# Output projection of a two-layer trunk: half columns of the gate loaded and summed piece by piece

## The chip, the cores and the metric

The kernel runs on one core of one Trainium2 chip. The metric is the device time of one execution in microseconds (us); lower is better. In the profile PE is the matrix engine, PEld its weight loads, DVE the vector engine, ACT the scalar engine, POOL the GpSimd engine, and SP the engine whose queue issues most transfers. Every engine works through its own instructions in a fixed order.

## The reference, cut to what matters

One sequence of 512 tokens with 2048 channels passes through two layers, an mLSTM layer and a band-attention layer, all in float32. Each layer ends in the same way; the part that the change touches is the end of the second one:

```python
sc = silu(c)                                            # (1, 2048)
mod = sc @ ada_w[l] + ada_b[l]                          # three blocks of 2048
shift, scale, gate = mod[:, :D], mod[:, D:2*D], mod[:, 2*D:]
...
y = (o * silu(z)) @ w_out                               # (512, 2048) @ (2048, 2048)
x = x + gate * rmsnorm(y, g_post[l])
```

So the last stage has two independent jobs: the product with `w_out`, and the gate of 2048 values, a matrix-vector product with 2048 x 2048 weights (16 MB). They meet where the product is multiplied with the gate, scaled by the row's norm and added to x.

## The kernel before

Products run on PE in float32 split into a high and a low part: each product of 128 x 128 by 512 columns is three matmuls. The weights come as pieces of 128 x 1024 (512 KB). `raw_load` issues a piece's load on SP into one of three buffers (`wr`, L259); `split` makes the high part with a cast on ACT and the low part with a subtraction on DVE, into one of three pairs (`wh`, L243). The subtraction ends the use of the load's buffer, so that the load of the piece three further on waits for it; the cast waits until PE is done with the piece three before.

The last stage (from L1552 on) computes the output in four groups of 512 columns, each in four banks of 128 tokens. `proj_b` takes a group through eight pieces of weights, k = 0, 2, ... 14. In groups 0 to 2 a piece serves all four banks with 24 matmuls (two blocks k by four banks by three), and the pieces are numbers 497 to 504, 505 to 512 and 513 to 520. Group 3 goes through its columns twice, for the token pairs (0, 1) and (2, 3), with 12 matmuls a piece: pieces 521 to 528 and 529 to 536. In the last pass the final three pieces are held and used bank by bank. There are five banks for this in turn, so that a group's second bank is one that the group before has to have emptied. `evac` empties a bank: DVE multiplies it with the gate row and writes `yo` (group 0 is copied, its gate comes later), and ACT squares it for the row's norm (`sqy`).

The gate is summed on DVE. `ada_load` loads a half column block (128 x 1024 of `adaT`, 512 KB, tile `ada`) and `ada_sum` (L550) multiplies it with silu(c), which stands as `scC` in all partitions, and sums along the row into one column of `mod`; a row that reads the accumulator follows each sum. There are 16 column blocks of two halves, 32 sums, taken in the order of blocks 84 to 95 and then 80 to 83, since group 0's gate is used last. Four buffers hold half columns. When a group's four blocks are summed, `gates_out` multiplies them with the norm's weights on DVE (`ggate`, L819), PE turns them into rows (`ps_gg`, L821), ACT copies them (L823), and SP writes them to `ggd`. `gate_row` then loads the row into all partitions, as `ssum` for groups 1 to 3 and as `gb0` for group 0. `gate_first` multiplies group 0's four outputs with `gb0`. `fetch_x` loads the residual of 128 tokens as two transfers of 512 KB. `finish` scales, adds and stores 128 tokens (four stores of 256 KB).

`gate_steps` says at which k of which group each of these steps is written into the program. Within an engine a scheduler may place an instruction earlier or later than the program does, by a priority, except that loads and sums of half columns keep their place among themselves and their neighbours roughly as written; the order that results is fixed when the program is built. Before, `gate_sums` works four half columns at a time: it sums the four that are loaded and issues the next four loads.

Of the kernel before, what the change touches and what calls it, by code (L numbers as in the profile page):

```python
# [187 lines left out]
def hybrid_trunk(ctx, tc, xT, xN, c, adaT, cols, wst, wg, ext, kc, out):  # L188
# [621 lines left out]
    def add_at(at, more):  # L810
        for k, f in more.items():
            at[k] = f if k not in at else lambda f=f, g=at[k]: (g(), f())
# [768 lines left out]
    def finish(m):  # L1581
        rs = row_rstd(m)
        if m in last:
            last[m]()
        for g in range(4):
            y = yo[m][g]
            nc.vector.scalar_tensor_tensor(y, y, rs, x2[m][g], op0=ALU.mult, op1=ALU.add)
            nc.sync.dma_start(out[m, :, g * S : (g + 1) * S], y)

    late, last = [], {}  # L1590
    gate_cols = [(80 + i, j) for i in [*range(4, KT), *range(4)] for j in range(2)]
    gate_in = []

    def gate_begin():
        late.append(op.tile([P, D], F32, tag="sc", name="scC", bufs=1))
        late.append(op.tile([P, S], F32, tag="gb", name="gb0", bufs=1))
        nc.sync.dma_start(late[0], csc.rearrange("a d -> (a d)").partition_broadcast(P))
        gate_sums()

    def gate_sums():  # L1600

        for a in gate_in:
            ada_sum(*a, tc.keep_in_program_order, late[0])
        gate_in[:] = [ada_load(i, op, 4, tc.keep_in_program_order, 2, [j]) for i, j in gate_cols[:4]]
        del gate_cols[:4]

    def gate_part(g):
        gates_out(1, 4 * g, 4 * g + 4, rp, bufs=1)

    def gate_first():  # L1610

        for m in range(4):
            nc.vector.tensor_tensor(yo[m][0], yo[m][0], late[1], op=ALU.mult)

    gate_steps = {
        0: {10: gate_begin},
        1: {0: gate_sums, 4: gate_sums, 8: lambda: gate_part(1), 10: gate_sums, 12: lambda: (gate_row(1, 1), fetch_x(0)), 14: gate_sums},
        2: {2: lambda: (gate_part(2), gate_sums()), 4: lambda: fetch_x(1), 6: lambda: (gate_row(1, 2), gate_sums()), 10: gate_sums, 12: lambda: (gate_part(3), fetch_x(2)), 14: gate_sums},
        3: {2: lambda: (gate_row(1, 3), fetch_x(3)), 4: lambda: gate_part(0), 8: lambda: gate_row(1, 0, late[1]), 12: gate_first},
    }  # L1620
    for g in range(4):
        for pair in [range(4)] if g < 3 else PAIRS:
            ps = [newp(f"ps_y1_{g}_{m}") for m in pair]
# [6 lines left out]
                    evac(p, m, g, yo[m][g], g > 0, last if g == 3 and pair == PAIRS[1] else None)  # L1630
    finish(2)
    finish(3)
    assert wpos[0] == len(order)
    ost.close()


# [57 lines left out]
```

## Time and profile before

| what | value |
|---|---|
| device time, three runs | 2645.3 us median (2644.92 to 2646.06) |
| the profiled execution | 2643.96 us, its span 2642.0 us |
| mean granted clock of PE | 0.996 |
| DVE, ACT, POOL busy | 88%, 54%, 2% of the span |
| stage of the last projection | PE's first `ps_y` of it at 2451.19 us, its last group of products from 2628.35 us |
| in that stage, PE waits by releaser | ACT `sqy` 3.2 us (2), DVE `wh` 1.6 us (2), ACT `wh` 0.3 us (1) |
| in that stage, DVE waits for half columns | 24.1 us in 12 waits; a sum takes 1.28 us |
| in that stage, ACT's casts wait for weights | 17.2 us in 9 waits |

The span runs from the first to the last instruction; the device time is measured around it. A row of the timeline has the start and the length in us, the engine, the line, the operation with its tiles and the number of instructions merged into it, and in brackets how long the engine was idle before it and what ended the wait. A row of busy time by stretches has, behind the stretch, its length, the busy time of PE, PEld, DVE, ACT and POOL with instruction counts, the granted clock, the busy share of the DMA engines and GB/s.

### The profile page before, as it was taken

Reading aid. Unit: us, or ns where it says so; the run is one execution under the profiler, and the core shown is the slowest. Engines: PE = TensorE matmul, PEld = TensorE weight load, DVE = VectorE, ACT = ScalarE, POOL = GpSimd, SP = SyncE. Lnnn points to the kernel's source line nnn. Section 1 sums busy time; section 2 is a strip of 40 time slices with the busy share of each in tenths; the row PEclk is TensorE's granted clock in tenths of the full one; section 3 lists DMA queues with packets and bytes.
Section 4 is the critical chain, followed back from the end, with each engine's and each line's share of the span. In section 5 each row is a group of like instructions: output and inputs, shape, how many; then the busy total and the mean of one; then the engine's idle time right before and its main releaser. Section 6 shows DMA issues by size and latency. Waiting matters only on the chain.

```text
span 2642.0 us, 45758 instructions
## 1 busy us (share of the span) xinstructions
PE 2579.1 (98%) x17994; PEld 2409.5 (91%) x17994; DVE 2337.3 (88%) x3812; ACT 1438.0 (54%) x2113; POOL 55.1 (2%) x110
## 2 busy tenths in 40 slices
PE   8999999999999999999999999999999999999998
PEld 6887888899999999999999998788999899999887
DVE  8978988999989999899998886877997999999666
ACT  4344533466556665566655453578443776677423
POOL 0000111000000000000000000000000000000000
PEclk9999999999999999999999999999999999999999
DMA  9766797433333333333337548878654534444687
GB/s 365 310 266 247 273 347 294 171 111 127 110 99 126 120 116 119 101 127 120 111 122 248 185 162 318 308 253 307 223 174 143 169 125 140 144 132 141 228 309 241
DMA packets 155825, 510.60 MB, mean 193 GB/s; under 512 B 17893, under 2 KB 31749, under 8 KB 141145
## 3 DMA queue, kind: packets, MB, share of 16 engines
q1 hardware_dynamic: 145498, 445.99, 49.2%
q0 software_dynamic: 10112, 61.70, 6.3%
q8 instruction: 141, 2.31, 0.4%
q14 instruction: 74, 0.61, 0.1%
HBM read 473.96 MB, written 38.90 MB: 194 GB/s over the span
## 4 chain that ended last, share of the span: by engine, by line
PE 57%; DVE 22%; issue 9%; DMA 7%; ACT 4%; POOL 0%; SPq 0%; DVEq 0%; ACTq 0%; POOLq 0%
DVE wh L243 6%; PE ps_azo L311 4%; PE ps_dzo L311 4%; PE ps_czo L311 4%; DVE ada L550 4%; PE ps_y_True L311 3%; PE ps_dz L311 3%; PE ps_cz L311 3%; PE ps_az L311 3%; PE ps_y L311 3%; PE ps_y_False L311 3%; DMA wr<-in_wst 2%; DMA ada<-in_adaT 2%; PE ps_bzo L311 2%; PE ps_s L311 2%
## 5 line engine op out<-in xcount | busy, mean ns | idle before, releaser
L243 ACT CAST wh<-wr 128x1024 fp32r<-128x1024 f32 (+1 forms) x536 | 553.4, 1034 | 453.0 <-DMA wr<-in_wst 97.5
L243 DVE TENSOR_TENSOR wh<-wr,wh 128x1024 fp32r<-128x1024 f32 (+1 forms) x536 | 644.4, 1205 | 118.0 <-ACT wh L243 117.2
L243 ACT CAST wsh<-ws 128x768 fp32r<-128x768 f32 (+1 forms) x296 | 241.7, 817 | 314.7 <-PE ps_az L311 67.4
L243 DVE TENSOR_TENSOR wsh<-ws,wsh 128x768 fp32r<-128x768 f32 (+1 forms) x296 | 277.6, 938 | 48.8 <-ACT wsh L243 48.1
L550 DVE CUSTOM_DVE_ANT_0 ada<-ada,scB,cl 128x2048 f32<-128x2048 f32 (+1 forms) x89 | 206.1, 2325 | 12.2 <-DMA ada<-in_adaT 11.8
L282 DVE TENSOR_TENSOR ws<-wr 128x512 f32<-128x512 f32 (+1 forms) x296 | 199.3, 675 | 6.2 <-DMA wr<-in_wst 5.8
L311 PE MATMUL ps_y<-wh,y 128*128 128x512 f32 x768 | 171.6, 384 | 5.2 <-ACT sqy L1161 3.2
L311 PE MATMUL ps_y_False<-wh,y 128*128 128x512 f32 x768 | 169.1, 381 | 3.0 <-DVE wh L243 2.7
L311 PEld LDWEIGHTS ps_y<-wh,y 128*128 128x128 f32 x768 | 145.0, 191 | 28.4 <-ACT sqy L1161 4.0
L311 PEld LDWEIGHTS ps_y_False<-wh,y 128*128 128x128 f32 x768 | 144.2, 189 | 25.7 <-DVE wh L243 5.0
L311 PE MATMUL ps_v<-wh,h 128*128 128x512 f32 x576 | 127.5, 380 | 0.0
L311 PE MATMUL ps_kv<-wh,hkv 128*128 128x512 f32 x576 | 126.5, 380 | 0.8 <-DVE wh L243 0.8
L284 DVE TENSOR_TENSOR ws<-wr 128x256 f32<-128x256 f32 (+1 forms) x296 | 122.8, 417 | 3.4
L283 DVE TENSOR_TENSOR wr<-ws,wr 128x256 f32<-128x256 f32 (+1 forms) x296 | 122.5, 416 | 2.5
L311 PEld LDWEIGHTS ps_kv<-wh,hkv 128*128 128x128 f32 x576 | 108.0, 189 | 17.0 <-DVE wh L243 1.8
L311 PEld LDWEIGHTS ps_v<-wh,h 128*128 128x128 f32 x576 | 108.2, 189 | 15.8 <-issue 0.9
L311 PE MATMUL ps_l<-h,wh 128*128 128x512 f32 x480 | 107.8, 380 | 2.1 <-DVE wh L243 2.1
L311 PEld LDWEIGHTS ps_l<-h,wh 128*128 128x128 f32 x480 | 90.2, 189 | 16.8 <-DVE wh L243 3.3
L311 PE MATMUL ps_azo<-h,wh 128*128 128x256 f32 (+1 forms) x606 | 92.9, 285 | 0.0
L311 PE MATMUL ps_y_True<-wh,y 128*128 128x512 f32 x384 | 83.3, 379 | 0.0
L311 PEld LDWEIGHTS ps_y_True<-wh,y 128*128 128x128 f32 x384 | 72.5, 189 | 10.3
L550 DVE CUSTOM_DVE_ANT_0 ada<-ada,scC,cl 128x2048 f32<-128x2048 f32 (+1 forms) x35 | 65.2, 1863 | 18.8 <-DMA ada<-in_adaT 18.8
(431 smaller groups left out, 5853.5 us busy)
## 6 DMA issues: line engine op xcount, KB each, us to landing
wr<-in_wst SPq DMA_DIRECT2D x506, 512.0 KB, 3.5
ada<-in_adaT POOLq DMA_DIRECT2D x57, 1024.0 KB, 7.1
ada<-in_adaT SPq DMA_DIRECT2D x49, 1024.0 KB, 7.0
ada<-in_adaT SPq DMA_DIRECT2D x36, 512.0 KB, 7.7
wr<-in_wst SPq DMA_DIRECT2D x26, 384.0 KB, 3.7
xt<-nsc SPq DMA_DIRECT2D x32, 256.0 KB, 3.6
yr<-ysc SPq DMA_DIRECT2D x28, 256.0 KB, 5.7
ysc<-zo SPq DMA_DIRECT2D x24, 256.0 KB, 4.1
```

The source lines that it names most:

```text
L243: ins = nc.scalar.copy(hi, src), nc.vector.tensor_tensor(lo, src, hi.bitcast(F32), op=ALU.subtract)
L282: nc.vector.tensor_tensor(t[:, : 2 * w], r[:, w : 3 * w], r[:, : 2 * w], op=ALU.subtract)
L283: nc.vector.tensor_tensor(r[:, w : 2 * w], t[:, w : 2 * w], r[:, :w], op=ALU.add)
L284: nc.vector.tensor_tensor(t[:, 2 * w :], r[:, 3 * w :], r[:, w : 2 * w], op=ALU.subtract)
L311: product[0] = nc.tensor.matmul(ps, a, b, start=start, stop=stop)
L550: pin(nc.vector.tensor_tensor_reduce(c, c, (sc or scB)[:, j * w : (j + 1) * w], 1.0, mod[:, i : i + 1] if j else col(CB + i), ALU.mult, AL ...
```

## The change

The 32 half columns are taken one at a time. `gate_sums(n)` does n steps; a step sums the oldest half column if four are under way (or if none is left to load) and issues one load. The first load comes at the second piece of group 0 (`gate_begin` moves from k = 10 to k = 2), and then one step follows per piece in group 0, one or two per piece in groups 1 and 2 (two where k is a multiple of 4), and 2, 2 and 1 in the first three pieces of group 3. The other steps move by one or two pieces, as `gate_steps` shows; `gate_first` multiplies two of group 0's outputs at k = 12 and two at k = 14. The stores of the first 256 tokens go from SP to POOL.

```diff
-            nc.sync.dma_start(out[m, :, g * S : (g + 1) * S], y)
+            (nc.gpsimd if m < 2 else nc.sync).dma_start(out[m, :, g * S : (g + 1) * S], y)
...
         nc.sync.dma_start(late[0], csc.rearrange("a d -> (a d)").partition_broadcast(P))
-        gate_sums()
-
-    def gate_sums():
-
-        for a in gate_in:
-            ada_sum(*a, tc.keep_in_program_order, late[0])
-        gate_in[:] = [ada_load(i, op, 4, tc.keep_in_program_order, 2, [j]) for i, j in gate_cols[:4]]
-        del gate_cols[:4]
+
+    def gate_sums(n=1):
+
+        for _ in range(n):
+            if len(gate_in) == 4 or not gate_cols:
+                ada_sum(*gate_in.pop(0), tc.keep_in_program_order, late[0])
+            if gate_cols:
+                i, j = gate_cols.pop(0)
+                gate_in.append(ada_load(i, op, 4, tc.keep_in_program_order, 2, [j]))
...
-    def gate_first():
-
-        for m in range(4):
+    def gate_first(m0):
+
+        for m in range(m0, m0 + 2):
             nc.vector.tensor_tensor(yo[m][0], yo[m][0], late[1], op=ALU.mult)
...
-        0: {10: gate_begin},
-        1: {0: gate_sums, 4: gate_sums, 8: lambda: gate_part(1), 10: gate_sums, 12: lambda: (gate_row(1, 1), fetch_x(0)), 14: gate_sums},
-        2: {2: lambda: (gate_part(2), gate_sums()), 4: lambda: fetch_x(1), 6: lambda: (gate_row(1, 2), gate_sums()), 10: gate_sums, 12: lambda: (gate_part(3), fetch_x(2)), 14: gate_sums},
-        3: {2: lambda: (gate_row(1, 3), fetch_x(3)), 4: lambda: gate_part(0), 8: lambda: gate_row(1, 0, late[1]), 12: gate_first},
+        0: {2: gate_begin},
+        1: {6: lambda: gate_part(1), 10: lambda: gate_row(1, 1), 12: lambda: fetch_x(0)},
+        2: {2: lambda: gate_part(2), 6: lambda: (gate_row(1, 2), fetch_x(1)), 12: lambda: (gate_part(3), fetch_x(2))},
+        3: {2: lambda: (gate_row(1, 3), fetch_x(3)), 6: lambda: gate_part(0), 8: lambda: gate_row(1, 0, late[1]), 12: lambda: gate_first(0), 14: lambda: gate_first(2)},
     }
+    for k in range(2, KT, 2):
+        add_at(gate_steps[0], {k: gate_sums})
+    for g in (1, 2):
+        gate_steps[g] = {k: lambda n=1 + (k % 4 == 0), f=gate_steps[g].get(k): (gate_sums(n), f and f()) for k in range(0, KT, 2)}
+    for k, n in ((0, 2), (2, 2), (4, 1)):
+        gate_steps[3][k] = lambda n=n, f=gate_steps[3].get(k): (gate_sums(n), f and f())
```

What the scheduler makes of it is seen in the order of instructions on each engine, at three places. In the names, `ada92_0` is the first half of column block 92, `wh515` the split of piece 515, `yo2_1` the output of token block 2 in group 1, and the number at a tile's end is its own. The rows that read the accumulator after each sum are left out.

On DVE at the end of group 1, before the change, from the split of piece 514 to that of 515:

```order
L243 TENSOR_TENSOR wh514_27615<-wr514_27613,wh514_27615 128x1024
L1158 TENSOR_TENSOR yo0_1_27546<-ps_y1_1_0_27251,ssum_108 128x512
L1158 TENSOR_TENSOR yo1_1_27550<-ps_y1_1_1_27252,ssum_108 128x512
L550 ISA ada92_0_27509,mod_103<-ada92_0_27509,scC_27113,cl_100 128x1024
L1158 TENSOR_TENSOR yo2_1_27554<-ps_y1_1_2_27253,ssum_108 128x512
L550 ISA ada92_1_27511,mod_103<-ada92_1_27511,scC_27113,mod_103 128x1024
L1158 TENSOR_TENSOR yo3_1_27558<-ps_y1_1_3_27254,ssum_108 128x512
L243 TENSOR_TENSOR wh515_27648<-wr515_27646,wh515_27648 128x1024
```

and after it, up to the gate product for columns 88 to 91:

```order
L243 TENSOR_TENSOR wh514_27609<-wr514_27607,wh514_27609 128x1024
L1158 TENSOR_TENSOR yo0_1_27543<-ps_y1_1_0_27260,ssum_108 128x512
L1158 TENSOR_TENSOR yo1_1_27547<-ps_y1_1_1_27261,ssum_108 128x512
L550 ISA ada93_0_27512,mod_103<-ada93_0_27512,scC_26965,cl_100 128x1024
L1158 TENSOR_TENSOR yo2_1_27551<-ps_y1_1_2_27262,ssum_108 128x512
L1158 TENSOR_TENSOR yo3_1_27555<-ps_y1_1_3_27263,ssum_108 128x512
L550 ISA ada91_1_27440,mod_103<-ada91_1_27440,scC_26965,mod_103 128x1024
L243 TENSOR_TENSOR wh515_27644<-wr515_27642,wh515_27644 128x1024
L550 ISA ada92_0_27473,mod_103<-ada92_0_27473,scC_26965,cl_100 128x1024
L819 TENSOR_TENSOR ggate_105<-mod_103,cl_100 128x4
```

One sum is left between the evictions instead of two, and it is of another half column. Before, the gate product stood ahead of the split of 513; now it stands behind that of 515. On SP the load of `ada92_0` stood right behind the load of piece 516, with those of `ada92_1` and `ada93_0` behind it; now the load of `ada93_0` stands alone right behind the load of piece 515.

On DVE at the end of group 2, before the change, from the last two sums on:

```order
L550 ISA ada83_0_27754,mod_103<-ada83_0_27754,scC_27113,cl_100 128x1024
L550 ISA ada83_1_27756,mod_103<-ada83_1_27756,scC_27113,mod_103 128x1024
L819 TENSOR_TENSOR ggate_105<-mod_103,cl_100 128x4
L243 TENSOR_TENSOR wh522_27901<-wr522_27899,wh522_27901 128x1024
L1158 TENSOR_TENSOR yo0_2_27859<-ps_y1_2_0_27562,ssum_108 128x512
L1158 TENSOR_TENSOR yo1_2_27863<-ps_y1_2_1_27563,ssum_108 128x512
L1158 TENSOR_TENSOR yo2_2_27867<-ps_y1_2_2_27564,ssum_108 128x512
L1158 TENSOR_TENSOR yo3_2_27871<-ps_y1_2_3_27565,ssum_108 128x512
L243 TENSOR_TENSOR wh523_27924<-wr523_27922,wh523_27924 128x1024
```

and after it, from the last eviction of group 2 to the same gate product:

```order
L1158 TENSOR_TENSOR yo3_2_27864<-ps_y1_2_3_27562,ssum_108 128x512
L550 ISA ada81_1_27744,mod_103<-ada81_1_27744,scC_26965,mod_103 128x1024
L243 TENSOR_TENSOR wh523_27918<-wr523_27916,wh523_27918 128x1024
L550 ISA ada82_0_27776,mod_103<-ada82_0_27776,scC_26965,cl_100 128x1024
L243 TENSOR_TENSOR wh524_27941<-wr524_27939,wh524_27941 128x1024
L550 ISA ada82_1_27779,mod_103<-ada82_1_27779,scC_26965,mod_103 128x1024
L243 TENSOR_TENSOR wh525_27959<-wr525_27957,wh525_27959 128x1024
L550 ISA ada83_0_27821,mod_103<-ada83_0_27821,scC_26965,cl_100 128x1024
L550 ISA ada83_1_27871,mod_103<-ada83_1_27871,scC_26965,mod_103 128x1024
L243 TENSOR_TENSOR wh526_27976<-wr526_27974,wh526_27976 128x1024
L819 TENSOR_TENSOR ggate_105<-mod_103,cl_100 128x4
```

Five sums and four splits have moved in between the last eviction and the gate product. On SP the load of `ada83_1`, the last half column, now stands behind the load of piece 526, which stands behind the load of `ssum` for group 3 and the first half of the residual of token block 3.

On PE in group 3 the transpose of that gate product stood, before, between pieces 522 and 523:

```order
L311 MATMUL ps_y1_3_0_27875<-wh522_27901,y2_1_1_26975 128x512 x3
L311 MATMUL ps_y1_3_1_27876<-wh522_27901,y2_1_1_26975 128x512 x3
L821 MATMUL ps_gg1_0_27917<-kcs_101,ggate_105 4x128
L311 MATMUL ps_y1_3_0_27875<-wh523_27924,y2_2_0_27009 128x512 x3
L311 MATMUL ps_y1_3_1_27876<-wh523_27924,y2_2_0_27009 128x512 x3
```

and stands after it within piece 525:

```order
L311 MATMUL ps_y1_3_0_27868<-wh524_27941,y2_3_1_27058 128x512 x3
L311 MATMUL ps_y1_3_1_27869<-wh524_27941,y2_3_1_27058 128x512 x3
L311 MATMUL ps_y1_3_0_27868<-wh525_27959,y2_4_0_27094 128x512 x3
L821 MATMUL ps_gg1_0_27934<-kcs_101,ggate_105 4x128
L311 MATMUL ps_y1_3_1_27869<-wh525_27959,y2_4_0_27094 128x512 x3
```

It has moved from 24 matmuls into group 3 to 51. At the end, on DVE, the split of piece 532 moves from behind the first two multiplies of `finish` to ahead of them; between the splits of 534 and 535 stood three of these multiplies before, and stand a reciprocal and three multiplies after the change.

More of the change, by code (lines that the diff above doesn't have):

```diff
@@ L1632, in hybrid_trunk @@
     finish(3)
-    assert wpos[0] == len(order)
+    assert wpos[0] == len(order) and not gate_cols and not gate_in
     ost.close()
```

## The prediction

> **What bounds the kernel now.** I read the page first, for the share of each engine.
>
> ```profile
> PE 2579.1 (98%) x17994; PEld 2409.5 (91%) x17994; DVE 2337.3 (88%) x3812; ACT 1438.0 (54%) x2113; POOL 55.1 (2%) x110
> ```
>
> PE is busy for 98% of the span, so a change that removes no matrix product can win only what PE loses in waits. I then read busy time by stretches, the stage before the changed one (2400 to 2450 us) beside the changed one.
>
> ```profile
> 2400.00:2450.00 50.00, 50.00 (x433) 49.68 (x433) 47.49 (x107) 35.16 (x65) 0.00 (x0) 1.00 0.50 152
> 2500.00:2550.00 50.00, 46.99 (x218) 40.66 (x218) 35.50 (x52) 12.69 (x21) 0.00 (x0) 1.00 0.84 292
> 2550.00:2600.00 50.00, 49.81 (x224) 42.76 (x223) 33.08 (x45) 14.77 (x24) 0.00 (x0) 0.97 0.87 294
> 2600.00:2642.00 42.00, 31.63 (x141) 25.94 (x139) 29.41 (x43) 15.28 (x23) 0.00 (x0) 0.96 0.65 217
> ```
>
> Up to 2450 us PE has no gap. In the last stage it loses about 3 us between 2500 and 2550, and the granted clock falls to 0.97 after it; DMA is busy 84 and 87% there against 50% before. The timeline of PE alone says where. In it a row's matmuls are counted, and the start of the next row shows what they really took.
>
> ```profile
> 2466.70 54.23 PE L311 MATMUL ps_y<-wh,y 128*128 128x512 f32 x250
> 2520.79 24.85 PE L311 MATMUL ps_y<-wh,y 128*128 128x512 f32 x114
> 2548.65 1.77 PE L311 MATMUL ps_y<-wh,y 128*128 128x512 f32 x6 [3.01 <-ACT sqy L1161]
> 2550.29 27.62 PE L311 MATMUL ps_y<-wh,y 128*128 128x512 f32 x120
> 2577.77 11.90 PE L311 MATMUL ps_y<-wh,y 128*128 128x512 f32 x54
> 2589.87 4.15 PE L311 MATMUL ps_y<-wh,y 128*128 128x512 f32 x18 [0.19 <-ACT sqy L1161]
> 2593.88 30.20 PE L311 MATMUL ps_y<-wh,y 128*128 128x512 f32 x138
> 2624.40 0.48 PE L311 MATMUL ps_y<-wh,y 128*128 128x512 f32 x1 [0.31 <-ACT wh L243]
> 2625.66 1.92 PE L311 MATMUL ps_y<-wh,y 128*128 128x512 f32 x6 [0.78 <-DVE wh L243]
> 2628.35 5.23 PE L311 MATMUL ps_y<-wh,y 128*128 128x512 f32 x23 [0.78 <-DVE wh L243]
> ```
>
> The undisturbed pace comes from the first two rows: 250 products in 2520.79 - 2466.70 = 54.1 us, 0.216 us each. Against it, from start to start: the 114 products take 27.9 instead of 24.6 us (3.2 lost); the next 6 + 120 take 29.1 instead of 27.2 (1.9 lost); the 54 and the 18 lose 0.5 together; the 138, 1, 6 and 23 at the end lose 0.7 + 1.0 + 1.4 + 0.3 = 3.4. That is 9.0 us in all, the ceiling of any gain in this stage, unless what follows the last product shrinks too. The second loss is the clock:
>
> ```profile
> 2545.50:2548.60 3.10, 0.14 (x1) 0.00 (x0) 2.62 (x4) 0.69 (x2) 0.00 (x0) 1.00 1.01 412
> 2550.30:2553.00 2.70, 2.70 (x9) 2.15 (x8) 2.67 (x4) 1.36 (x4) 0.00 (x0) 0.50 0.70 214
> ```
>
> An idle stretch of about 3 us (2545.6 to 2548.65) is followed by a granted clock of 0.50 for 2.7 us, in which 9 products run instead of 12. So the middle gap costs 3.2 + 1.9 = 5.1 us.
>
> [...] The row decides for this execution, and I keep 5.1.
>
> What PE waits for at the middle gap stands on DVE, ACT and SP:
>
> ```profile
> 2531.64 0.33 SPq L259 DMA_DIRECT2D wr<-in_wst  x1
> 2537.22 1.37 SPq L544 DMA_DIRECT2D ada<-in_adaT  x3
> ...
> 2539.44 0.68 DVE L1158 TENSOR_TENSOR yo<-ps_y,ssum 128x512 f32<-128x512 f32 x1
> 2545.98 1.28 DVE L550 CUSTOM_DVE_ANT_0 ada<-ada,scC,cl 128x1024 f32<-128x1024 f32 x1 [5.86 <-DMA ada<-in_adaT]
> 2547.19 0.69 DVE L1158 TENSOR_TENSOR yo<-ps_y,ssum 128x512 f32<-128x512 f32 x1
> 2547.91 0.58 ACT L1161 ACTIVATE sqy<-ps_y 128x512 f32<-128x512 f32 x1 [5.02 <-DVE yo L1158]
> ```
>
> The eviction of group 1's third bank (2547.19) stands on DVE behind a column sum, which waits 5.86 us for its half column: issued first of three at 2537.22, landed at 2545.98, 8.7 us. PE's group 2 needs that bank for its fourth product chain, after 18 products.
>
> **The change, part by part.** No product, sum, split or byte is added or removed; 32 half-column loads, 32 sums and 8 output stores move.
>
> *Sums from the second piece on.* At the middle gap the half column between the evictions is now 93's first half, and its load stands on SP right behind wr515, which waits for the split of piece 512. Before, that place was reached at 2531.64 (the row above), so at that pace the load is issued at about 2532.1, 5.2 us earlier than the one it replaces. Even with the same 8.7 us it lands at 2540.8. DVE reaches the sum when the second eviction ends (2539.44 + 0.68 = 2540.1); PE needs the bank 18 products into group 2, at 2545.5; sum and eviction take 1.3 + 0.6, and PE went on 0.7 after the square began (2547.91, 2548.65). So the sum may start as late as 2542.8, and the gap goes: **-5.1 us**, with the bounds 0 and -5.1. What is late next is a new one. PE's transpose of gate columns 88 to 91 keeps its place, 24 products into group 2 (2546.8), but its operand now comes behind the sum of 93, two evictions, a second sum, a split and a third sum: 3 x 1.3 + 2 x 0.6 + 1.2 + 0.1 = 6.4 us after the first starts, 2547.2 from 2540.8. Taken as **+0.3 us**, bounds 0 and 2.
>
> The two small losses at the start of group 3 (0.5) come from group 2's evictions, which before stood behind two waiting sums. In the new order three splits stand ahead of them and no sum: **-0.4**.
>
> *Five sums after group 2.* Before, all sums and the last gate product of DVE end before group 2 does. Now five sums stand between the last eviction of group 2 and the last gate product, with four splits among them, and PE's last transpose stands 51 products into group 3, in order, with products behind it.
>
> ```profile
> 2500.24 0.69 DVE L1160 COPY yo<-ps_y 128x512 f32<-128x512 f32 x1 [0.60 <-PE ps_y L311]
> 2573.69 1.28 DVE L550 CUSTOM_DVE_ANT_0 ada<-ada,scC,cl 128x1024 f32<-128x1024 f32 x1
> 2576.23 1.22 DVE L243 TENSOR_TENSOR wh<-wr,wh 128x1024 fp32r<-128x1024 f32 x1
> 2587.18 0.16 DVE L819 TENSOR_TENSOR ggate<-mod,cl 128x4 f32<-128x4 f32 x1
> ...
> 2593.86 0.27 PE L821 MATMUL ps_gg<-kcs,ggate 128*4 128x128 f32 x1
> ```
>
> Let T be the start of group 3 on PE. The last eviction ends at about T + 0.7 (as at group 0, first row). Five sums with their accumulator reads are 5 x 1.30, four splits 4 x 1.20, so the gate product is done at T + 12.1; PE stands at the transpose at T + 51 x 0.216 = T + 11.0. It waits **1.1 us at least**; before, the operand was 6.7 us ahead (2587.18 against 2593.86). The last of the five sums also needs its load. On SP that load stands behind the load of ssum, which waits for the last eviction, behind 512 KB of x and behind wr526, which waits for the split of 523; so it is issued at T + 0.7 + 1.3 + 1.2 + 0.4 = T + 3.6, and DVE is there at T + 0.7 + 4 x 1.3 + 3 x 1.2 = T + 9.5. It has 5.9 us to land.
>
> ```profile
> DMA to landing us min/median/max: 5.6/7.7/11.7
> SPq L1150 <- DVE yo L1158: 2.0, 1, 2.0
> ...
> 2593.29 5.54 DMA wr<-in_wst
> ```
>
> The 32 loads of this stage landed after 5.6, 7.7 and 11.7 us (least, median, most). The same wr526 in the same company (ssum and x ahead of it) took 5.5 us. The new load follows wr526 directly, with fewer column loads around it than the median one had. I take 7.2 us, between the nearest row and the median: 1.3 late, so the wait is **+2.4 us**. The ends are 1.1 (5.6 us) and 6.9 (11.7 us). Above about 3 us the clock row above adds 1.6 or so.
>
> What hides the other 24 sums in groups 1 and 2: a piece lasts 24 x 0.216 = 5.2 us there, and DVE needs one split and one or two sums for it (2.5 to 3.8 us). At most four loads are under way, so one group's twelve bear a landing time of up to about 12 us. Three sums in group 0 stand in DVE's idle time of 2470 to 2490, beside splits that are wanted about 8 us later. With that cover gone (loads at the maximum), one piece would come late by a sum or two, 1 to 3 us.
>
> *First group's gating in two steps, outputs on POOL.* The four products with gb0 take the same time; three now stand ahead of the split of piece 530. The end is this:
>
> ```profile
> 2615.73 1.00 SPq L1588 DMA_DIRECT2D out<-yo  x2
> 2621.07 2.07 DVE L1587 SCALAR_TENSOR_TENSOR yo<-yo,rsn,x 128x512 f32<-128x512 f32 x3
> 2623.30 1.05 ACT L243 CAST wh<-wr 128x1024 fp32r<-128x1024 f32 x1 [3.96 <-DMA wr<-in_wst]
> ...
> 2618.66 7.23 DMA wr<-in_wst
> ...
> 439.85 0.53 POOL L544 DMA_DIRECT2D ada<-in_adaT  x1 [9.41 <-DVE mod L550]
> ```
>
> Before, the last two weight loads were issued at 2617.5 and 2618.66, each when a split freed its buffer, not when SP was done with the stores (2615.73, over at 2616.7). Taking the stores off SP wins nothing by itself, and an issue on POOL costs 0.53 us of an idle engine. What moves is the order on DVE: the split of 532 now stands ahead of the reciprocal and the first multiplies, so wr535 is issued earlier and its 5.7 us are covered. Then the order itself is late: between the splits of 534 and 535 stand a reciprocal and three multiplies (0.15 + 2.07 us, second row), with the split 3.4 us, while PE spends 6 products, 1.3 us, on piece 534 in the first of its two banks. If 534 is just in time, 2.1 us are lost there instead of 3.4: **-1.3**, bounds 0 and -3.4. The chain behind the last product is as before.
>
> Sum: -5.1 + 0.3 - 0.4 + 2.4 - 1.3 = **-4.1 us**. The profiled execution took 2643.96 us, its span 2642.0 and 1.96 around it; that makes 2639.9. The median of the runs shown is 1.34 above the profiled one, so I forecast 2645.3 - 4.1 = **2641.2 us**. A measurement of this kernel can tell about 0.2%, 5.3 us, from no change: I forecast a gain just inside that bound.
>
> **The rivals.**
>
> 1. *All covered* (14%). The last half column lands in time and DVE keeps ahead of the end: -5.1 - 0.4 + 1.1 - 3.4 = -7.8, 2637.5 us. For it: DMA has less to do at once. Against it: three multiplies ahead of a split.
> 2. *The new wait halves the clock* (20%). At the median landing of 7.7 us the wait is 2.9, at 8.5 us it is 3.7; with 1.6 of clock the sum is -5.1 + 0.3 - 0.4 + 5.3 - 1.3 = -1.2, 2644.1 us. For it: the row at 2550.30. [...]
> 3. *The middle gap stays* (7%): 93's half column is late as 92's was. It must land after 2542.8, 10.7 us from issue, which the maximum of 11.7 allows. Sum +0.3 - 0.4 + 2.4 - 1.3 = +1.0, 2646.3 us.
> 4. *Slower* (9%): the last half column lands so late that the new wait outweighs the old one. With the clock, that is from a wait of 5.2 us on (5.2 + 1.6 = 5.1 + 0.4 + 1.3), so from a landing time of 10.0 us. At 11.7 us: 6.9 + 1.6 - 6.8 = +1.7, 2647.0 us; if the loads of x and weights behind each other at T cost more than any row shows, over 2650.6.
> 5. *Stores on a second queue hold up the last weights* (8%). DMA moved 217 GB/s on average over the last 42 us, and wr536 took 7.23 us while stores ran beside it. If stores from another queue take turns with it sooner, the 1.3 is not won, and wr536 lands as late as before: 2642.5 us, up to 2646. [...]
>
> **How the numbers follow.** My case has 42%: waits of 1.1 to 3 us, 2639.9 to 2641.8 us; a quarter of it lies under 2640.0. Faster by over 0.2%: rival 1 and that quarter, 0.25. Slower by over 0.2% (over 2650.6): 0.07, the far part of rivals 4, 3 and 5. Within: 0.68. The range leaves out the best of rival 1 and the far half of 3 and 4: 2637.4 to 2646.6.
>
> **What would show it.** PE's timeline must run from group 1 into group 2 without a gap and with the clock at 1.00; a gap there, with DVE waiting for a half column between the evictions, is rival 3. At the last transpose PE must wait for DVE's gate product 1 to 3 us; no wait refutes my new term, over 3 us with a clock of 0.5 behind it is rival 2 or 4, and the landing time of the last half column says which. At the end the casts should wait less for weights, and PE for splits behind three multiplies. If it is wrong, the likeliest reason is the landing time at the start of group 3, then a split that comes late in group 1 or 2.

## The result, and the profile after

The changed kernel takes **2640.32 us** (median of 22 runs, 2635.68 to 2646.44) beside 2644.73 us of the kernel before (22 runs, 2637.68 to 2650.03): a ratio of **0.9984, 95% interval 0.9978 to 0.9991**, or 4.2 us less (2.4 to 5.8). The forecast was 4.1 us less and 2641.2 us. Two later comparisons of the same changed kernel gave 0.9990 (0.9977 to 1.0002) and 1.0000 (0.9988 to 1.0012). Weighted by the inverse squares of their half-widths (0.00065, 0.00125, 0.0012), the three give 0.9988, 0.9983 to 0.9993: 3.2 us less, give or take 1.3. A gain is there, and it is below the 0.2% (5.3 us) that the prediction took as the bound of what one measurement can tell.

The profiled execution took 2643.82 us with a span of 2642.1, no shorter than the 2642.0 of before, though the last stage lost its gap. The timeline of PE alone shows the stage (start, duration, count of matmuls, and in brackets the idle time before the row with what ended it); these rows answer to those of before from 2466.70 on.

```profile
2457.86 2.19 PE L311 MATMUL ps_y<-wh,y 128*128 128x512 f32 x9
...
2473.36 49.05 PE L311 MATMUL ps_y<-wh,y 128*128 128x512 f32 x226
...
2522.28 31.33 PE L311 MATMUL ps_y<-wh,y 128*128 128x512 f32 x144
...
2553.47 26.15 PE L311 MATMUL ps_y<-wh,y 128*128 128x512 f32 x120
...
2579.48 21.61 PE L311 MATMUL ps_y<-wh,y 128*128 128x512 f32 x99
2602.43 0.27 PE L821 MATMUL ps_gg<-kcs,ggate 128*4 128x128 f32 x1 [1.33 <-DVE ggate L819]
2602.45 25.71 PE L311 MATMUL ps_y<-wh,y 128*128 128x512 f32 x118
2628.41 5.23 PE L311 MATMUL ps_y<-wh,y 128*128 128x512 f32 x23 [0.24 <-DVE wh L243]
```

Group 1 runs into group 2 inside the row of 144 products, which takes 2553.47 - 2522.28 = 31.2 us, 0.2166 each: the gap of 3.0 us is gone and the slow stretch behind it too. The one wait left is 1.33 us at the last transpose of gate columns, for DVE's gate product. From the first product of this stage to the last row of 23 it is 2628.41 - 2457.86 = 170.55 us, beside 2628.35 - 2451.19 = 177.16 before. So the stage is 6.6 us shorter and began 6.7 us later. What stands ahead of it on every engine is the same, instruction by instruction. The busy time by stretches of both kernels (before first; PE, PEld, DVE, ACT and POOL, then the clock, the share of DMA and GB/s) shows where the start was lost:

```profile
0.00:500.00 500.00, 477.75 (x2173) 402.46 (x2174) 440.26 (x520) 213.83 (x298) 38.11 (x76) 1.00 0.78 295
```

```profile
0.00:500.00 500.00, 472.76 (x2142) 398.20 (x2143) 434.17 (x507) 210.89 (x293) 38.13 (x76) 0.99 0.78 294
2500.00:2550.00 50.00, 50.00 (x234) 43.67 (x233) 32.36 (x45) 14.88 (x25) 0.00 (x0) 1.00 0.75 262
2550.00:2600.00 50.00, 50.00 (x234) 43.63 (x233) 33.42 (x48) 15.07 (x25) 0.00 (x0) 1.00 0.86 301
2600.00:2642.00 42.00, 32.07 (x148) 27.11 (x146) 30.75 (x46) 15.58 (x24) 4.34 (x8) 0.95 0.70 231
```

In the first 500 us PE worked on 2142 matmuls in the changed kernel and on 2173 before, and was busy 5.0 us less. This early part, with DMA at 78%, is the same program in both; over the 14 profiles of this study the last stage starts anywhere between 2450.7 and 2460.0 us, in kernels of either order. One profile of each can therefore not give the gain by its span. The length of the last stage leaves that start out. In the same rows the clock is now 1.00 from 2550 to 2600 (0.97 before) and PE has no gap from 2500 to 2600.

What DVE waits for, and the landing times of the 32 half columns (least, median, most), show that the loads are better covered and land sooner than the 24.1 us in 12 waits and 5.6/7.7/11.7 of before:

```profile
  DVE ada L550: 8.4, 7
...
DMA to landing us min/median/max: 3.8/6.7/9.6
```

### The profile page after: what moved, and what is told of

It is laid out like the page before. It is cut to its first block, busy times and chain, and to the rows that moved or that the text cites. A ratio compares the mean times of both kernels' runs of the same rounds, so it can differ in the third digit from the quotient of the medians.

```text
span 2642.1 us, 45759 instructions
## 1 busy us (share of the span) xinstructions
PE 2575.3 (97%) x17994; PEld 2407.0 (91%) x17994; DVE 2335.6 (88%) x3812; ACT 1436.6 (54%) x2113; POOL 59.5 (2%) x118
## 4 chain that ended last, share of the span: by engine, by line
PE 56%; DVE 24%; issue 8%; DMA 6%; ACT 5%; POOL 0%; SPq 0%; DVEq 0%; ACTq 0%; POOLq 0%
DVE wh L243 6%; PE ps_y L311 5%; PE ps_dzo L311 4%; PE ps_czo L311 4%; PE ps_azo L311 4%; DVE ada L550 3%; PE ps_cz L311 3%; PE ps_dz L311 3%; PE ps_y_True L311 3%; PE ps_y_False L311 3%; PE ps_az L311 3%; DMA wr<-in_wst 2%; PE ps_bzo L311 2%; DVE wsh L243 2%; DVE cv L793 2%
## 5 line engine op out<-in xcount | busy, mean ns | idle before, releaser
L550 DVE CUSTOM_DVE_ANT_0 ada<-ada,scB,cl 128x2048 f32<-128x2048 f32 (+1 forms) x89 | 205.7, 2320 | 12.5 <-DMA ada<-in_adaT 12.5
L311 PEld LDWEIGHTS ps_azo<-h,wh 128*128 128x128 f32 x606 | 79.3, 192 | 1.1
```

The lines of the kernel that those rows point to most:

```text
L311: product[0] = nc.tensor.matmul(ps, a, b, start=start, stop=stop)
L550: pin(nc.vector.tensor_tensor_reduce(c, c, (sc or scB)[:, j * w : (j + 1) * w], 1.0, mod[:, i : i + 1] if j else col(CB + i), ALU.mult, AL ...
```

## The experiments

All twelve are told by the last stage of their profile: its length from the first product of the last projection to the start of the row of 23, and what PE lost in it against 0.2163 us a product (250 in 54.07 us). "Behind the transpose" is the loss from the last transpose of gate columns to the row of 23. Before, the losses were 5.0 (middle gap with its clock; the prediction's rounder pace gave 5.1), 0.5 at the start of group 3 and 3.1; after, 1.6 at the transpose and 0.4 behind it.

### The same kernel again

No edit. The question was whether the two parts of the profiled result, the small wait and the small loss behind it, come back.

> The changed kernel once more. The last stage is measured from PE's first product of the last projection to the start of its last row of 23 products: 177.2 us before, 170.6 us after in the profiles at hand, 168.5 us with no wait at all. Theory: the gain comes from the order of the instructions, so it repeats: no gap at the start of group 2, a wait of 1 to 3 us at the last transpose, 0 to 1 us lost in the tail, stage 170 to 172 us, time 3 to 6 us under the kernel before. Rival: the 6.6 us were one lucky execution; then the wait at the last transpose is over 3 us or the tail loses its 3 us again, stage over 173 us, time less than 2.5 us under the kernel before.

```profile
2581.66 21.61 PE L311 MATMUL ps_y<-wh,y 128*128 128x512 f32 x99
2605.63 0.27 PE L821 MATMUL ps_gg<-kcs,ggate 128*4 128x128 f32 x1 [2.36 <-DVE ggate L819]
2605.66 27.40 PE L311 MATMUL ps_y<-wh,y 128*128 128x512 f32 x118
2633.57 5.23 PE L311 MATMUL ps_y<-wh,y 128*128 128x512 f32 x23 [0.51 <-DVE wh L243]
```

```profile
2606.20:2609.60 3.40, 3.40 (x10) 2.67 (x9) 0.52 (x1) 0.14 (x1) 0.00 (x0) 0.51 0.71 245
```

The wait was 2.36 us, and the clock was 0.51 for the next 3.4 us, in which 10 products ran, beside 17 in the third profile below: from the transpose to the row of 23 it was 27.9 us instead of 25.5, of which the clock is 1.7 (3.4 us at half rate). The stage took 173.5 us, over the 170 to 172 that were expected; the comparison gave the 0.9990 above. What differed from the first profile was the landing of the last half column, as the chain of waits has it in the first profile and in this one:

```profile
2593.56 6.17 DMA ada<-in_adaT
```

```profile
2595.74 7.20 DMA ada<-in_adaT
```

7.20 - 6.17 = 1.03 us of landing, 2.36 - 1.33 = 1.03 us of wait. The third profile of this kernel tests whether the landing sets the wait.

> The changed kernel a third time, beside the two above on the same chip. Theory: the wait at the last transpose is set by the landing of the last half column and differs between executions: 1.3 to 2.5 us, stage 170.5 to 171 us without and 173 to 174.5 us with the halved clock behind it; time 2 to 6 us under the kernel before and 1 to 4 us over gate_late. Rival: the order alone sets it; then the stage is within 0.5 us of one of the two profiles at hand by the wait alone, with no tie to the landing time (6.2 and 7.2 us there).

The landing was 7.24 us and the wait 2.40, again to the hundredth, and here the clock did not fall:

```profile
2601.15 0.27 PE L821 MATMUL ps_gg<-kcs,ggate 128*4 128x128 f32 x1 [2.40 <-DVE ggate L819]
2601.18 30.94 PE L311 MATMUL ps_y<-wh,y 128*128 128x512 f32 x141
```

```profile
2601.20:2604.60 3.40, 3.40 (x17) 3.00 (x18) 1.15 (x2) 1.30 (x2) 0.00 (x0) 1.00 0.63 192
```

So the stage took 171.4 us. That the wait goes with the landing held; that such a wait always halves the clock did not. The comparison gave 1.0000, where 2 to 6 us less were expected; its interval leaves room for 3.2 us. One comparison of 12 runs can thus miss a gain of this size.

### The kernel before again

No edit. Is the middle gap a fixed price of the old order?

> The kernel before against itself, with a profile of its own. It tells two things. First the last stage of the kernel before in a third execution (177.2 us, and 177.1 us with only the stores moved). Theory: the middle gap is set by the order and repeats, about 3 us with the halved clock behind it, stage 176 to 178 us. Rival: it is as much a matter of landing times as the wait of the changed kernel; then the gap is under 2 us or the clock stays at 1.00, stage 172 to 175 us, and the mean gain is smaller than the first pair of profiles says. Second the measurement: the ratio should be 1.000 with an interval of about 0.0012 to both sides, and the medians of two sets of a dozen runs may lie 2 us apart. The start of the stage, whose instructions before it are the same in all these kernels, should lie between 2450 and 2460 us, as in the twelve profiles so far.

```profile
2553.91 1.56 PE L311 MATMUL ps_y<-wh,y 128*128 128x512 f32 x6 [1.88 <-ACT sqy L1161]
...
2594.87 4.15 PE L311 MATMUL ps_y<-wh,y 128*128 128x512 f32 x18 [1.62 <-ACT sqy L1161]
```

```profile
2553.90:2557.30 3.40, 3.39 (x16) 2.91 (x17) 3.38 (x6) 1.77 (x4) 0.00 (x0) 1.00 0.89 347
```

It is not. The column was there sooner (DVE stood 4.74 us for it, 5.86 in the first profile), the gap shrank by 1.1 us to 1.88, and the clock stayed at 1.00, so 2.2 us were lost in place of 5.0; 1.62 were lost at the start of group 3, where the first profile lost 0.19. The stage took 174.9 us. Against itself the kernel before gave 1.0006 (0.9995 to 1.0017).

### The middle gap alone

On the kernel before, the sum at the end of group 1 is taken out and put at the start of group 2; nothing else of the change.

```
-        1: {0: gate_sums, ... 12: lambda: (gate_row(1, 1), fetch_x(0)), 14: gate_sums},
-        2: {2: lambda: (gate_part(2), gate_sums()), ...
+        1: {0: gate_sums, ... 12: lambda: (gate_row(1, 1), fetch_x(0))},
+        2: {0: gate_sums, 2: lambda: (gate_part(2), gate_sums()), ...
```

> The kernel before, with the sums of one step moved from the last piece of group 1 to the first of group 2, so that no sum stands between the evictions of group 1; nothing else of the change. Theory: the middle gap and the slow clock behind it go (-5.1 us), PE waits about 0.6 us for the gate product of columns 88 to 91 (four sums and two splits now stand ahead of it, 8.4 us after group 1 against 36 products, 7.8 us), the tail loses its 3.4 us as before: stage about 172.7 us, time about 4.5 us under the kernel before. Rival: the gain of the change comes from the spread of the loads or from the tail; then the stage stays at 175 us or more. Second rival: the eight sums that now crowd into pieces 516 to 519 make splits late, 1 to 3 us lost within group 2.

```profile
2522.62 28.74 PE L311 MATMUL ps_y<-wh,y 128*128 128x512 f32 x132
...
2600.52 8.04 PE L311 MATMUL ps_y<-wh,y 128*128 128x512 f32 x36 [0.46 <-DVE wh L243]
2610.22 14.60 PE L311 MATMUL ps_y<-wh,y 128*128 128x512 f32 x66 [1.66 <-DVE wh L243]
2625.59 1.68 PE L311 MATMUL ps_y<-wh,y 128*128 128x512 f32 x6 [0.76 <-DVE wh L243]
2628.04 5.23 PE L311 MATMUL ps_y<-wh,y 128*128 128x512 f32 x23 [0.78 <-DVE wh L243]
```

```profile
2608.34 0.69 DVE L1613 TENSOR_TENSOR yo<-yo,gb 128x512 f32<-128x512 f32 x1 [4.23 <-DMA gb<-ggd]
```

The gap is gone (132 products in one row), and 2.9 us of it come back: 0.5 at the transpose in group 2 (a wait of 0.30), 0.6 more than before up to the transpose in group 3 (a wait of 0.70), and in the rest of group 3 waits of 0.46, 1.66, 0.76 and 0.78 for splits, 4.9 us behind the transpose against 3.1 before. The stage took 175.0 us, where 172.7 were expected and the rival had 175 or more; the time ratio was 1.0003 (0.9991 to 1.0016). DVE stood 4.23 us at the first multiply with the gate row gb0, whose store and load wait on SP behind pieces that wait for splits; the splits of the next pieces stood behind it. In this order of group 3 the middle gap was not worth its 5.0 us.

### The five sums earlier

On the changed kernel, four of the five sums behind group 2 go into it, so that one is left there and its load is issued earlier.

```
-        ... n=1 + (k % 4 == 0) ...
+        ... n=1 + (k % 4 == 0 or g == 2 and k in (2, 6, 10, 14)) ...
-    for k, n in ((0, 2), (2, 2), (4, 1)):
+    for k, n in ((0, 1),):
```

> The changed kernel with two steps per piece in all but the first pieces of group 2, so that four of the five sums behind group 2 are done ahead of it. Theory: the wait at the last transpose (1.4 us) goes, the start of group 2 stays without a gap. DVE's order at the end is that of the kernel before again (a multiply with the gate row ahead of the split of 528, two of the final multiplies ahead of that of 532). If that order cost the tail, 2.9 us come back there: stage 172.0 us. If the tail was lost to weights that stood behind column loads, it stays under 1 us: stage 169.2 us, time about 1.4 us under the changed kernel. Rival: two sums in each piece of group 2 make a split late, 1 to 3 us lost within group 2.

The wait at the transpose was gone, and 2.2 us were lost behind it instead of 0.4, with DVE standing 2.16 us at the gate row:

```profile
2604.28 0.69 DVE L1615 TENSOR_TENSOR yo<-yo,gb 128x512 f32<-128x512 f32 x1 [2.16 <-DMA gb<-ggd]
```

Stage 171.2 us, between the 172.0 and 169.2 of the two accounts; 2641.35 us, ratio 0.9985 (0.9974 to 0.9997): no better than the changed kernel. The wait was thus not simply lost time. ACT's casts waited 16.7 us for weights here and 4.4 us in the changed kernel, so the weights come later. That they come in while PE stands at the transpose is one account; the old order of DVE's multiplies, which this kernel has again, is the other, and this run doesn't separate them.

### The outputs on POOL alone, and back on SP

On the kernel before, `nc.sync` becomes `(nc.gpsimd if m < 2 else nc.sync)` for the output stores; on the changed kernel the reverse.

> The kernel before with the stores of the first 256 tokens on POOL, nothing else. Theory: no change, since SP was done with these stores before the last splits freed a buffer: stage 176 to 178 us, the last two weights issued as before, about 16 us and 14.7 us ahead of the end of PE. Rival: the stores on SP are what makes the last weights late; then the tail loses under 1 us and the stage is 174.3 us. Second rival: stores of a second queue slow the last weights, which then land after 8 us and more, stage over 178 us.

> The changed kernel with all stores on SP, as before the change. Theory: POOL's stores change nothing: stage 170 to 174 us, as the two profiles of the changed kernel (170.6 and 173.5), by the wait at the last transpose (1.3 to 2.4 us) and whether the clock halves behind it; at most 1 us lost in the tail. Rival: the tail was cured by POOL's stores; then it loses 2 to 3 us here.

POOL alone: gap of 2.87 us, after which six products took 2.7 us instead of 1.3, 2.7 us lost behind the transpose, stage 177.07 us beside 177.16. Back on SP: wait of 2.47 us (landing 7.31) with the clock at 0.53 behind it, stage 174.13; without the 1.7 us of the clock 1.2 us were lost behind the transpose, half a microsecond above the 0.2 to 0.7 of the three profiles of the changed kernel and just over the 1 us expected. The stores' queue has no effect that these runs, one profile of each, can tell. The eight issues on POOL took 4.34 us in all (the row from 2600 above), 0.54 each.

### The last block of x later

On the changed kernel, and on the one with the sums earlier, `fetch_x(3)` is moved from the start of group 3 to its end.

```
-        3: {2: lambda: (gate_row(1, 3), fetch_x(3)), ...
+        3: {2: lambda: gate_row(1, 3), ...
...
+    fetch_x(3)
     finish(2)
```

> The changed kernel with the residual of token block 3 (two transfers of 512 KB) loaded behind the last weights instead of at the start of group 3; PE and DVE keep their order. The last half column is then issued ahead of the load of piece 526 and with no residual ahead of it. Theory: the wait at the last transpose has two parts, DVE's own work (1.1 us) and the landing of the last half column (0.3 us in the first profile, 1.3 us and a halved clock in the second). The second part goes: it lands within 6 us of its issue at 2 us into group 3, before DVE is there (9.5 us), the wait is 1.0 to 1.2 us and the clock stays at 1.00 behind it; stage 170.0 to 170.6 us. Rival: the landing time is that of a loaded DMA and not of the two transfers ahead; then DVE waits for it again and the wait is 1.3 us or more. Second rival: the transfers hold up the last weights or the end of the kernel in their new place; then over 14 us lie between the start of the last row of 23 products and the end of the span (13.7 us so far), or the tail loses over 1 us.

> The kernel of early5 (no sums but one behind group 2, no wait at the last transpose, 2.2 us lost behind it to late splits) with the residual of token block 3 loaded behind the last weights. PE and DVE keep the order of early5, whose end is that of the kernel before. Theory: in group 3 a piece is used every 2.6 us while its load, cast and split need 6 to 8 us for three pieces, so that what is late at the start of the group stays late to its end; the residual ahead of piece 526 made it late. Without it, it lands 1.4 us sooner (one transfer of 512 KB), and the 2.2 us fall to under 1 us: stage 169.0 to 170.0 us. Rival: the order of DVE at the end makes the loss; then it stays at 2 us and more, stage 171 us. Second rival, as before: over 14 us behind the start of the last row.

On the changed kernel the wait at the transpose fell to 0.57 us, DVE's own part (no sum waits for a landing there), with 0.9 lost behind it: stage 170.2 us as expected, ratio 0.9990 (0.9979 to 1.0001).

```profile
2600.98 0.27 PE L821 MATMUL ps_gg<-kcs,ggate 128*4 128x128 f32 x1 [0.57 <-DVE ggate L819]
```

On the other the expectation fell: 3.3 us behind the transpose, stage 172.25, ratio 0.9990 (0.9980 to 1.0000). Its 1.4 us for one transfer of 512 KB is an estimate: it fits the 378 GB/s of full DMA engines that 295 GB/s at a share of 0.78 come to (first 500 us, before). DVE stood longer at the first multiply with the gate row:

```profile
2603.59 0.69 DVE L1615 TENSOR_TENSOR yo<-yo,gb 128x512 f32<-128x512 f32 x1 [5.11 <-DMA gb<-ggd]
```

> As early5_x3, with the last gate product's store, load and multiplies written one piece later, which moves the first multiply with the gate row on DVE from ahead of the split of 528 to behind it, and the last pair apart. Theory (late weights at the start of group 3): no change against early5_x3, within 0.5 us. Rival (the order on DVE): what early5_x3 still loses in the tail goes here, over 0.5 us less.

With the gate part two steps later and both multiplies behind it (`8: gate_part(0)`, `12: (gate_row(1, 0, late[1]), gate_first(0))`) DVE still stood 3.56 us at the gate row. Stage 172.7 us, within the 0.5 us of the kernel above that was expected, but otherwise made up: 2.9 us were lost behind the transpose and 0.9 in a wait at the start of group 3. It is no way out, since the row's load moved with its use.

### The multiplies with the gate row behind the weights

On the kernel with the sums earlier, the multiplies are moved into the second pass of group 3 and held there in program order; in the second kernel the last block of x is late as well.

```
-  ... 12: lambda: gate_first(0), 14: lambda: gate_first(2)},
+  ...},
-  at = {4: lambda: finish(0), 6: lambda: finish(1)} ...
+  at = {2: lambda: (gate_first(0),), 4: lambda: (finish(0), gate_first(2),), 6: lambda: (finish(1),)} ...
```

> The kernel of early5 with the four multiplies of group 0 by its gate row held back on DVE: the first two behind the split of 529 (before: from ahead of the split of 528 on), the other two behind that of 533. PE and SP keep the order of early5. Theory, formed on the last runs: what the kernels without a wait at the last transpose lose in group 3 is DVE standing at the first of these multiplies until the gate row has landed (2.2 us in early5, 5.1 and 3.6 us in the two kernels with the residual moved, 1.4 us in the kernel before), with the splits behind it. Then DVE waits for the row no more and less than 1 us is lost behind the last transpose instead of 2.2: stage 169.0 to 169.9 us, time 4 to 8 us under the kernel before. Rival: the weights themselves are late in group 3, whatever DVE does; then over 1.5 us stay, stage 170.5 us or more. Second rival: the two multiplies that now lie between the last splits make those late, and the loss only moves to the last 40 products.

> As gate_late, with the residual of token block 3 loaded behind the last weights (the only difference). Theory: with DVE no longer held up, the residual ahead of piece 526 is worth at most the lateness that is left, so 0 to 0.8 us less than gate_late: stage 168.7 to 169.5 us. Rival: none of it shows, stage within 0.2 us of gate_late, as the weights are ahead of PE either way.

```profile
2592.31 21.18 PE L311 MATMUL ps_y<-wh,y 128*128 128x512 f32 x97
...
2623.09 5.23 PE L311 MATMUL ps_y<-wh,y 128*128 128x512 f32 x23 [0.90 <-DVE wh L243]
```

```profile
2600.79 28.95 PE L311 MATMUL ps_y<-wh,y 128*128 128x512 f32 x133
2630.03 5.23 PE L311 MATMUL ps_y<-wh,y 128*128 128x512 f32 x23 [0.29 <-DVE wh L243]
```

DVE's wait at the gate row is gone in both. The first still loses 2.0 us behind the transpose (133 products in 30.78 us), with x ahead of the piece that comes late, whose load took 7.10 us. Its stage took 171.5 us, as the rival of late weights had it, and the casts waited 15.4 us for weights; so DVE's stand at the gate row is not the only cause. The second loses 0.5 (29.24 us). Its stage took 170.5 us, over the 168.7 to 169.5 expected, with a 1.14 us wait at the start of group 3 for a column that was 10.2 us under way. The ratios were 0.9987 (0.9976 to 0.9998) and 0.9989 (0.9977 to 1.0001). The loss behind the transpose thus falls to half a microsecond here only with both causes gone. Part of the 1.5 us between the two may be that later start, if it gives the weights time; one profile of each doesn't separate it.

No kernel tried is clearly faster than the changed one.

## Why the prediction was right, step by step

**The sum was right, and more on average than in the one profile.** Four profiles of stages with the changed order (the three of the changed kernel and the one with its stores on SP) took 170.55, 173.54, 171.4 and 174.13 us, 172.4 on average; three with the old order (two of the kernel before, one with stores on POOL) 177.16, 174.89 and 177.07, 176.4 on average. The difference is 4.0 us, beside 4.1 forecast. The parts differ more: in the first profile the five terms below came to -5.0 + 0 - 0.5 + 1.6 - 2.7 = -6.6 us, as measured, against -5.1 + 0.3 - 0.4 + 2.4 - 1.3. On average over the seven profiles they came to -4.0 + 0 - 1.1 + 2.4 - 2.1, and +0.8 for a slow clock that was not in the sum. Errors of up to 1.1 us cancel in it, and the gain itself is measured only to within 1.3 us; that the sum agrees to 0.1 us is partly luck.

1. *Middle gap, -5.1.* Right in mechanism and for its own execution: the column of the old order came late, and in the new order the sum between the evictions (L550, first row) has no wait:

```profile
2546.71 1.27 DVE L550 CUSTOM_DVE_ANT_0 ada<-ada,scC,cl 128x1024 f32<-128x1024 f32 x1
2547.91 1.28 DVE L1158 TENSOR_TENSOR yo<-ps_y,ssum 128x512 f32<-128x512 f32 x2
...
2552.65 0.15 DVE L819 TENSOR_TENSOR ggate<-mod,cl 128x4 f32<-128x4 f32 x1
```

   The gap never came back in the eleven profiles in which the sum had been moved. Its size is not fixed: 3.01, 2.87 and 1.88 us in three profiles of the old order, 5.0, 4.8 and 2.2 us with the clock, so the forecast took nearly the largest. Rival 3 did not occur.
2. *Gate product of group 2, +0.3.* It came in time: it was done at 2552.8 (last row above), and the transpose at 2553.44 stands in the profile without a wait. Nothing was lost.
3. *Start of group 3, -0.4.* The first profile lost nothing there, 0.5 less than before; the other two profiles of the old order lost 1.9 and 1.0, and none of the four with the changed order lost anything.
4. *Last transpose, +2.4.* The mechanism was right, and its formula close: 1.1 + (landing - 5.9) is landing - 4.8, and the measured wait is landing - 4.84 in all four profiles (6.17 and 1.33, 7.20 and 2.36, 7.24 and 2.40, 7.31 and 2.47). The landing of 7.2 that was taken is met in three of them; the first profile happened to have 6.17. DVE's own floor was put too high: 1.1 was forecast, and 0.57 is left where the landing is no longer last.

   DVE's timeline of the first profile: the fifth sum (L550) starts 0.82 us late, and the gate product (L819) stands behind it and one split more, as forecast.

```profile
2598.96 0.08 DVE L550 DVE_READ_ACCUMULATOR2_ANT mod<- 128x1 f32 x1
2599.87 1.28 DVE L550 CUSTOM_DVE_ANT_0 ada<-ada,scC,mod 128x1024 f32<-128x1024 f32 x1 [0.82 <-DMA ada<-in_adaT]
...
2602.22 0.15 DVE L819 TENSOR_TENSOR ggate<-mod,cl 128x4 f32<-128x4 f32 x1
```

5. *The end, -1.3.* **This is the step that was mis-sized**: "If 534 is just in time, 2.1 us are lost there instead of 3.4". The loss behind the transpose went from 3.1 us to 0.4, so by 2.7, within its bounds and twice the value taken. (The prediction's 3.4 counts 0.3 for the row of 23 itself, which lasts 5.23 us in every profile that shows it and is no loss.)

```profile
2609.61 1.90 DVE L1615 TENSOR_TENSOR yo<-yo,gb 128x512 f32<-128x512 f32 x3
...
2621.77 1.22 DVE L243 TENSOR_TENSOR wh<-wr,wh 128x1024 fp32r<-128x1024 f32 x1
...
2623.10 2.08 DVE L1587 SCALAR_TENSOR_TENSOR yo<-yo,rsn,x 128x512 f32<-128x512 f32 x3
2625.09 1.22 DVE L243 TENSOR_TENSOR wh<-wr,wh 128x1024 fp32r<-128x1024 f32 x1
...
2627.13 1.23 DVE L243 TENSOR_TENSOR wh<-wr,wh 128x1024 fp32r<-128x1024 f32 x1 [0.16 <-ACT wh L243]
```

   These are the multiplies with the gate row (first) and, from the second row on, the splits of 534 and 535 with the reciprocal's multiplies between them. The row of 23 starts with the first product that needs the low part of 536; the first that needs that of 535 stands 6 products ahead, and that of 534 12 products ahead, here at 2626.7 and 2625.4. The split of 534 was done at 2621.77 + 1.22 = 2623.0, so it was 2.4 us early, not just in time. The three multiplies do stand between the two splits as forecast. They use up most of that lead, and cost nothing: the split of 535 was done at 2626.3, 0.4 us before PE needed it (before, PE waited 0.78 us for it, at 2625.66). What ends last now is the load of the last piece, on the chain of waits of the same profile, with its cast and split behind it:

```profile
2620.56 5.39 DMA wr<-in_wst
...
2626.05 1.06 ACT wh L243
...
2627.13 1.24 DVE wh L243
```

   In the second profile the chain runs instead through the multiplies and the split of 535, as forecast, with 0.7 us lost apart from the clock.

   Where the lead comes from was not in the working. Before, ACT's casts stood waiting for weights in group 3; after, they hardly did, as the prediction's signs have it (total in us, times, longest; before first):

```profile
ACT wh L243 <- DMA wr<-in_wst: 17.2, 9, 4.0
```

```profile
ACT wh L243 <- DMA wr<-in_wst: 4.4, 2, 2.2
```

   Before, DVE stood 1.41 us at the first multiply with the gate row and PE had no wait over 0.78 us in group 3; after, the first multiply stands behind two splits more, DVE doesn't wait (2609.61 has no bracket), and PE itself waits 1.33 us at the transpose, which could give the loads time. 4.9, 2.2, 3.3 and 2.9 us were lost behind the transpose where DVE stood 4.23, 2.16, 5.11 and 3.56 us at the gate row, and 0.2 to 0.9, apart from the clock, in the changed kernel and the one with x late, where it didn't stand there; the run with stores on SP had 1.2. But 2.0 us were lost with the multiplies held back and x early, where it didn't stand there either. The split of 534 was 2.4 us early in all five profiles with the changed order of DVE, whether PE had waited 0.57 or 2.47 us, so the length of that wait doesn't set the lead. How much of it is due to DVE's order and how much to PE's wait is not shown. Rival 1's end was nearly met in the first profile (0.4 us left), its landing was not.
6. *Rival 2, the new wait halves the clock.* It happened in two of the four profiles with this order, at waits of 2.36 and 2.47 us, and cost 1.7 us each time. The prediction let the clock fall only above a wait of about 3 us; that bound was wrong. The rival had 20%; by these four profiles it deserved about half. The later comparisons with smaller gains would fit it, but nothing shows which of their runs had it.
7. *First group's gating in two steps; stores on POOL.* No run has the two steps alone, so that they cost nothing is not shown. The stores were priced at nothing by themselves, and both runs agree with it; the last piece's load took 5.39 us after the change and 6.17 with POOL alone, beside 7.23 before, so rival 5 did not occur.
8. *The reference point.* The sum was taken against a median that was 1.3 us above the profiled run. The 22 runs of the kernel before beside the changed one had a median of 2644.73, 0.6 lower than that of the three runs shown. The time was forecast to 0.9 us, and the difference to 0.1 by the ratio or 0.3 by the medians (4.4 us).

## What to carry to other kernels

Price a gap together with what stands behind it: taking out the largest wait alone brought no gain that could be measured here, as part of the loss came back behind it. Removing a wait of PE can move the loss rather than end it: with the sums earlier 1.6 us went at the transpose and 1.8 came back behind it. That weights come in during such a wait is one account of this, not shown. Where the run-to-run spread is as large as the gain, compare the length of the changed stage over several profiles, not the span of one.

## What was not expected of the hardware

**The clock after a short gap.** All gaps of the last stage of 1.8 us and more, from the 14 profiles: 1.88 us (clock stays at 1.00), 2.36 (0.51), 2.40 (stays), 2.47 (0.53), 2.87 (half), 3.01 (0.50). The same kernel at 2.36 and 2.40 us came out on both sides, so the length of the gap doesn't decide alone. The early part shows the same within one execution, the first profile of the changed kernel: behind a gap of 2.25 us that ended at 260.81 the clock was 0.50 from 261.8 to 265.2, and behind one of 2.70 us that ended at 321.31 it was 1.00 for the next 3.4 us. The slow stretch was about 3.4 us there and in the last stage before (0.50 from 2549.9 to 2553.3), and in the last stage it cost 1.7 to 1.8 us. What decides beside the length of the gap is not shown: no run here moved a gap of one length to another place.

**The landing of one load.** The same 512 KB load at the same place of the same program, issued behind the same loads, took 6.17, 7.20 and 7.24 us in three executions. On a path where the wait is landing minus a constant, that microsecond is the result.
